# Layer 0's gate/up projection as seven products of 2x2 blocks in place of eight

## The chip, the cores and the metric

The kernel runs on one core of a Trainium2 chip. The metric is the device time of one execution in microseconds (us). The kernel before the change took 1969.73 us, the median of three runs (1968.4 to 1976.09).

## The reference

Two layers of a trunk over 512 latent tokens and 256 context tokens, with 1024 features, all in float32. The change concerns the feed-forward part (FFN) of layer 0, which both streams pass through:

```python
def swiglu(h, w_in, w_out):
    gt, up = jnp.split(h @ w_in, 2, axis=-1)
    return (jax.nn.silu(gt) * up) @ w_out
...
x = x + g_f * swiglu(hf, ffn_w_in[l], ffn_w_out[l])
ctx = ctx + cg_f * swiglu(hcf, ffn_w_in[l], ffn_w_out[l])
```

`hf` and `hcf` are the RMS-normalised streams, scaled and shifted by vectors that come from the conditioning (adaLN: `silu(c) @ ada_w[l] + ada_b[l]`). The hidden width is 2816, that is 22 tiles of 128. The up projection `h @ w_in` gives a gate half and an up half of 2816 each; the down projection `@ w_out` goes back to 1024. Ahead of the FFN of layer 0 lies its mixer (attention and a delta rule), which ends with an output projection; behind it lies layer 1.

## The kernel before

**Precision.** Every large product is made of three matmuls in a reduced float32 format: each operand is split into a high part and the rest, and `mm3` (L178) adds high x high, high x low and low x high. Splitting costs one operation on ACT (the rounded copy, L164 for weights) and one subtraction on DVE (L165). Weights come in by `wstage` (L155): a tile `st` of up to 128 x 1024 is taken from a pool of **two** buffers and loaded by a DMA that SP issues; `whi` and `wlo`, its two parts, have three buffers each.

**The FFN of layer 0** (`ffn(kx, x, 0, ...)`). Tokens lie along the columns: 256 of the context, then 512 latent ones. The 22 hidden tiles are taken in four groups of 6, 5, 6 and 5 (`GROUPS`). For each tile of a group, two weight tiles are loaded (gate and up, 512 KB each), and for each of the two segments (256 and 512 columns) `up` (L1422) runs 24 matmuls for the gate and 24 for the up half; ACT takes the silu, DVE the product, and the result is split into `mh` and `ml`. Then `down` (L1439) multiplies the group's tiles for each of the 8 output tiles c and adds the result to `x` on DVE (L1447). In the last group the down stage of five output tiles is run segment by segment in three segments of 256, so that the norm of layer 1 (class `Norm`, `acc` and `finish`) can start on a segment that is complete.

**The norm.** `acc` squares a tile on ACT and sums on DVE or POOL. `finish` sums over partitions with two matmuls (`sp`, L329), takes a reciprocal root in some dozen small operations (on POOL for the norms here, L192 to L204), spreads it over the partitions with two more matmuls (`rb`, L335), and then scales each of the eight tiles (DVE L338) and splits it (ACT L346, DVE L347). Layer 0's FFN norm runs inside the loop `out2` (L1343): for each of three segments the last part of the output projection, then `finish`.

**Rows of layer 1's adaLN** are computed meanwhile on DVE. `ada_rows` (L275) loads one row tile of 512 KB at a time into a buffer `ast` of its own (two of them, L1402) and multiplies it by the silu of the conditioning with a running sum (L281). There are 48 rows; the first 16 are done twice, for both streams. `ada_step` puts one row ahead of each weight load, until all are done.

**What sets the order.** The program is written as above, and a scheduler orders each engine's instructions when the kernel is built, by priorities and a simulated timeline. On the chip each engine, and each DMA queue, takes its instructions strictly in that order; a wait holds all that stands behind it.

## Time and profile before

| | us |
|---|---|
| median of three runs | 1969.73 |
| lowest, highest | 1968.4, 1976.09 |
| the profiled execution, its own time | 1970.71 |
| its span, first to last instruction | 1968.7 |
| PE's busy time up to 696 us (layer 0's mixer) | 593.64 |
| PE's busy time from 1300 us on (layer 1) | 654.43 of 668 |

The mean granted TensorE clock of the profiled execution was 0.975. Everything about durations below comes from this one execution, whose own time is 1 us over the median.

How to read the lines. In a row of the timeline stand the start in us, the duration, the engine, the line of the program, the operation and its output and inputs; a wait that the profile shows follows in brackets. In a table by stages stand a stretch of the span, its length, then the busy time (and the number of instructions) of PE, of PE's weight loads, DVE, ACT and POOL, the granted clock, the share of the DMA engines in use and GB/s. In the chain of waits stand the start and length of a piece, its engine and line. A row of groups has the shapes and count, then the busy time and the mean of one in ns. A DMA row has the number of transfers, their size and the median time from issue to landing.

### The profile page before, as it was taken

How to read it: one execution, taken by the hardware profiler on the slowest of the kernel's cores; microseconds unless marked ns; L12 is line 12 of the kernel's file. 1: busy time of each engine (PE TensorE's matmuls, PEld its weight loads, DVE VectorE, ACT ScalarE, POOL GpSimd, SP SyncE). 2: the span in 40 equal slices, each digit the busy share in tenths (PEclk: the TensorE clock that was granted, in tenths of full speed). 3: DMA queues.
4: the chain of work that ended last, by engine and by line, in shares of the span. 5: the costliest groups of instructions: out<-in, count | busy, mean ns of one | idle time of the engine just before them, and what ended most of it. 6: DMA issues, size and time to landing. Idle time of an engine off the chain costs nothing.

```text
span 1968.7 us, 30208 instructions
## 1 busy us (share of the span) xinstructions
PE 1832.6 (93%) x11670; PEld 1625.2 (83%) x11670; DVE 1086.1 (55%) x2453; ACT 745.8 (38%) x1682; POOL 260.5 (13%) x360
## 2 busy tenths in 40 slices
PE   4978999688988979999999999999999989999999
PEld 3857889677877869888888888989999778888887
DVE  6566688786777585544444332546655663334333
ACT  3434454446574342212122122446555443222221
POOL 2122214441200050000000000420110020000000
PEclk8988999899999979999999999999999989999999
DMA  7456644656444723344443111211211213323232
GB/s 295 152 178 199 203 133 149 182 158 201 122 147 137 235 103 129 120 147 125 123 150 100 61 65 53 88 54 55 70 55 45 86 34 100 107 79 114 87 107 95
DMA packets 105215, 238.41 MB, mean 121 GB/s; under 512 B 10896, under 2 KB 48016, under 8 KB 103920
## 3 DMA queue, kind: packets, MB, share of 16 engines
q1 hardware_dynamic: 92544, 208.31, 33.3%
q0 software_dynamic: 4064, 14.38, 2.5%
q10 hardware_dynamic: 8464, 13.79, 2.0%
q8 instruction: 92, 1.51, 0.3%
q14 instruction: 51, 0.42, 0.1%
HBM read 203.44 MB, written 32.99 MB: 120 GB/s over the span
## 4 chain that ended last, share of the span: by engine, by line
PE 75%; DVE 8%; DMA 8%; ACT 3%; issue 3%; POOL 2%; SPq 0%; ACTq 0%; POOLq 0%; DVEq 0%
PE f L178 46%; PE d L178 16%; PE o L178 2%; DMA qkd<-ar 1%; PE vp L470 1%; PE sc L1582 1%; PE o L1607 1%; PE S L1172 1%; DMA MB<-md 1%; PE m L876 1%; DMA md<-dec 1%; PE t L1200 1%; DVE cv L373 1%; PE m L1596 1%; DMA st<-in_ada_w_dram 1%
## 5 line engine op out<-in xcount | busy, mean ns | idle before, releaser
L164 ACT ACTIVATE whi<-st 128x1024 fp32r<-128x1024 f32 (+4 forms) x219 | 212.2, 970 | 598.5 <-PE f L178 440.9
L165 DVE TENSOR_TENSOR wlo<-st,whi 128x1024 fp32r<-128x1024 f32 (+4 forms) x219 | 246.5, 1126 | 258.7 <-ACT whi L164 254.7
L178 PE MATMUL f<-hhi,whi 128*128 128x512 f32 (+1 forms) x1088 | 381.0, 352 | 3.0 <-ACT hhi L346 3.0
L178 PE MATMUL f<-hlo,whi 128*128 128x512 f32 (+1 forms) x1088 | 382.0, 352 | 1.1 <-DVE hlo L347 1.1
L178 PE MATMUL f<-hhi,wlo 128*128 128x512 f32 (+1 forms) x1088 | 381.1, 351 | 0.0
L178 PE MATMUL d<-whi,hhi 128*128 128x256 f32 (+1 forms) x800 | 234.5, 295 | 22.9 <-ACT ar L209 16.6
L178 PE MATMUL d<-wlo,hhi 128*128 128x256 f32 (+1 forms) x800 | 232.6, 292 | 1.3 <-DVE wlo L165 1.3
L178 PEld LDWEIGHTS f<-hhi,whi 128*128 128x128 f32 x1088 | 208.3, 192 | 30.0 <-ACT hhi L346 3.6
L178 PEld LDWEIGHTS f<-hlo,whi 128*128 128x128 f32 x1088 | 208.8, 192 | 28.1 <-DVE hlo L347 1.6
L178 PE MATMUL d<-whi,hlo 128*128 128x256 f32 (+1 forms) x800 | 231.7, 291 | 0.0
L178 PEld LDWEIGHTS f<-hhi,wlo 128*128 128x128 f32 x1088 | 208.8, 192 | 26.2
L178 PEld LDWEIGHTS d<-whi,hhi 128*128 128x128 f32 x800 | 156.5, 196 | 28.7 <-ACT ar L209 17.8
L178 PE MATMUL f<-ml,whi 128*128 128x512 f32 (+1 forms) x478 | 169.7, 356 | 0.0
L178 PE MATMUL f<-mh,whi 128*128 128x512 f32 (+1 forms) x478 | 169.1, 356 | 0.0
L178 PE MATMUL f<-mh,wlo 128*128 128x512 f32 (+1 forms) x478 | 168.8, 356 | 0.0
L178 PEld LDWEIGHTS d<-wlo,hhi 128*128 128x128 f32 x800 | 156.6, 196 | 2.5 <-DVE wlo L165 1.7
L178 PEld LDWEIGHTS d<-whi,hlo 128*128 128x128 f32 x800 | 156.0, 196 | 1.2
L1447 DVE SCALAR_TENSOR_TENSOR x<-f,scal,x 128x256 f32<-128x256 f32 (+1 forms) x101 | 64.1, 639 | 142.9 <-PE f L178 142.8
L1435 DVE TENSOR_TENSOR sg<-f,sg 128x512 f32<-128x512 f32 (+1 forms) x68 | 40.1, 589 | 166.4 <-PE f L178 162.6
L318 POOL TENSOR_TENSOR ssq<-ssq,sq 128x256 f32<-128x256 f32 x39 | 32.1, 825 | 648.0 <-ACT sq L316 647.3
L178 PE MATMUL d<-hhi,whi 128*128 128x512 f32 (+1 forms) x304 | 107.2, 353 | 4.0 <-ACT cin L209 2.2
L178 PE MATMUL d<-hhi,wlo 128*128 128x512 f32 (+1 forms) x304 | 105.3, 347 | 0.0
(378 smaller groups left out, 3454.9 us busy)
## 6 DMA issues: line engine op xcount, KB each, us to landing
st<-in_wfi_dram SPq DMA_DIRECT2D x88, 512.0 KB, 3.5
ast<-in_ada_t_dram SPq DMA_DIRECT2D x48, 512.0 KB, 4.3
st<-in_ada_w_dram SPq DMA_DIRECT2D x32, 512.0 KB, 3.7
st<-in_wfo_dram SPq DMA_DIRECT2D x32, 384.0 KB, 3.0
st<-in_wfo_dram SPq DMA_DIRECT2D x32, 320.0 KB, 2.9
aw<-in_ada_dram SPq DMA_DIRECT2D x8, 1024.0 KB, 12.3
st<-in_w1kv_dram SPq DMA_DIRECT2D x16, 512.0 KB, 3.3
aqT<-qkd SPq DMA_DIRECT2D x48, 128.0 KB, 3.7
```

The costliest lines, as they stand in the source:

```text
L164: S.activation(out=hi, in_=st, func=AF.Copy)
L165: last_lo[:] = [V.tensor_tensor(out=lo, in0=st, in1=hi.bitcast(F32), op=ALU.subtract).ins]
L178: r = T.matmul(out=ps, lhsT=p, rhs=q, start=(c == 0), stop=(c == n - 1))
L318: (V if k >= self.on_v else G).tensor_tensor(out=self.ssq[i], in0=self.ssq[i], in1=sq, op=ALU.add)
L373: V.scalar_tensor_tensor(out=cv, in0=cin[:, i:i + 772], scalar=convw[:, tix, i:i + 1], in1=cv, op0=ALU.mult, op1=ALU.add)
L470: T.matmul(out=vp[i, s], lhsT=w[:, ws], rhs=h[k][:, sl], start=(k == 0 and q == 0), stop=(k == KT - 1 and q == 2),)
L876: T.matmul(out=ps[:, i, :], lhsT=lhs[:, c, :], rhs=rhs[:, c, :], start=True, stop=True)
L1172: T.matmul(out=ps[:, o:o + w], lhsT=u.q[:, part, :], rhs=kst[:, m, sl], start=(i == 0), stop=(i == 1))
L1200: T.matmul(out=ov, lhsT=PT[:, i, :], rhs=vt[:, u.kts[i], :], start=(i == 0), stop=(i == u.nk - 1))
L1435: V.tensor_tensor(out=sg, in0=pss[1], in1=sg, op=ALU.mult)
L1447: V.scalar_tensor_tensor(out=o, in0=ps, scalar=scal[l, "g_f", s][:, c:c + 1], in1=o, op0=ALU.mult, op1=ALU.add,)
L1582: T.matmul(out=o, lhsT=lq[:, q], rhs=kv(lk), start=(i == 0), stop=(i == 2))
```

## The change

Layer 0 gets an FFN of its own, `ffn0`; `ffn` now serves layer 1 alone.

**Seven products.** The two weight tiles of a hidden tile form a matrix of 2 x 2 blocks: gate and up (rows) by the two halves of the features, 512 each. The normalised stream forms another: the two halves of the features by two halves of the tokens, 384 columns each (context 0 to 127 with latent 0 to 255, and context 128 to 255 with latent 256 to 511). The variant of Strassen's scheme used here takes sums of blocks on both sides, and needs seven products of blocks where the plain way has eight: 7 x 12 matmuls of 384 columns a tile.

**On the tokens' side**, once per layer: class `NormS` puts the normalised stream into four tiles `hf`. Its method `half` splits blocks b11 and b21 after the second segment (`half(0)`), and after the third (`half(1)`) makes t1, T2 (DVE), T3 and T4 (POOL), and splits T2, T1, T3, b22 and T4.

**On the weights' side**, for each tile: POOL makes four sums of 512 columns (tiles `ws`), and there are four splits (gate, two sum tiles, block a22) where there were two. The seven products are added up on DVE in tiles `ev`.

**The rows** of adaLN no longer have `ast` buffers; they are loaded by `wstage` into the same two buffers `st` that the weights use. Each row is taken in two halves of 512. One row comes with each odd tile (from the second group on) and one ahead of each output tile in the down stages.

**The groups** are six: 4, 4, 4, 4, 3 and 3 tiles (`GROUPS0`). The number of buffers of the work tiles is changed accordingly, `whi` and `wlo` stay at three. The layout of `w_out` follows the groups.

```diff
...
+GROUPS0 = [(0, 4), (4, 4), (8, 4), (12, 4), (16, 3), (19, 3)]
+HALF = 384
...
         def ada_rows(l, b, ns, stage, cbc, junk):
...
             for j in range(16):
                 st = stage(a["ada_t"][l, 16 * b + j], 1024)
                 for s in range(ns):
-                    r = V.scalar_tensor_tensor(
-                        out=junk if s < ns - 1 else st, in0=st, scalar=1.0, in1=cbc[:, s, :], op0=ALU.mult, op1=ALU.mult,
-                        accum_out=sc[:, s, j:j + 1],
-                    )
-                    tc.add_manual_dep(r.ins, last_lo[0].name, after, reason="pace")
+                    for i in range(2):
+                        cs = slice(512 * i, 512 * i + 512)
+                        r = V.scalar_tensor_tensor(
+                            out=junk() if s < ns - 1 else st[:, cs], in0=st[:, cs], scalar=1.0, in1=cbc[:, s, cs],
+                            op0=ALU.mult, op1=ALU.mult, accum_out=part[:, s, i, j:j + 1],
+                        )
+                        tc.add_manual_dep(r.ins, last_lo[0].name, after, reason="pace")
                 yield 0, 0
...
+                V.tensor_tensor(out=sc[:, s, :], in0=part[:, s, 0, :], in1=part[:, s, 1, :], op=ALU.add)
...
+        class NormS(Norm):
...
+            def put(self, k, s, sl, t):
+                if self.hf is None:
+                    self.hf = [self.fp.tile([128, 2, 2, HALF], F32, name="hf", tag="mid", bufs=5) for _ in range(4)]
+                d = self.hf[k // 2][:, k % 2]
+                if sl.start == 0:
+                    d, t = d[:, :, 0:128], t.rearrange("p (g n) -> p g n", g=2)
+                else:
+                    d = d[:, sl.start // 256 - 1, 128:HALF]
+                S.activation(out=d, in_=t, func=AF.Identity, bias=self.sv[s][:, k:k + 1])
...
+            def split(self, name, q, src):
+                hi, lo = self.parts(name, q)
+                S.activation(out=hi, in_=src, func=AF.Copy)
+                V.tensor_tensor(out=lo, in0=src, in1=hi.bitcast(F32), op=ALU.subtract)
+                self.var.setdefault(name, []).append((hi, lo))
+            def half(self, i):
+                def b(kh, n, q):
+                    return self.hf[2 * kh + q][:, :, n, :]
+                if i == 0:
+                    for kh, name in enumerate(("b11", "b21")):
+                        for q in range(2):
+                            self.split(name, q, b(kh, 0, q))
+                    return
+                t1 = [self.fp.tile([128, 1024], F32, name="t1", tag="ws", bufs=2)[:, 0:2 * HALF].rearrange("p (z n) -> p z n", z=2) for _ in range(2)]
+                for q in range(2):
+                    V.tensor_tensor(out=t1[q], in0=b(0, 1, q), in1=b(0, 0, q), op=ALU.subtract)
+                    t2 = b(0, 0, q)
+                    V.tensor_tensor(out=t2, in0=b(1, 1, q), in1=t1[q], op=ALU.subtract)
+                    self.split("T2", q, t2)
+                for q in range(2):
+                    self.split("T1", q, t1[q])
+                    G.tensor_tensor(out=b(0, 1, q), in0=b(1, 1, q), in1=b(0, 1, q), op=ALU.subtract)
+                for q in range(2):
+                    self.split("T3", q, b(0, 1, q))
+                    G.tensor_tensor(out=b(1, 0, q), in0=b(1, 0, q), in1=b(0, 0, q), op=ALU.subtract)
+                for q in range(2):
+                    self.split("b22", q, b(1, 1, q))
+                for q in range(2):
+                    self.split("T4", q, b(1, 0, q))
...
+        if q:
+            kx.n0.half(q - 1)
...
+            junk = lambda: gs.tile([128, 512], F32, name="junk", tag="C")
             for b in range(3):
-                yield from kx.ada_rows(1, b, 1 if b else 2, astage, cbc, junk)
-
-        ada_it = adas() if l == 0 else iter(())
+                yield from kx.ada_rows(1, b, 1 if b else 2, kx.wstage, cbc, junk)
...
+        def weights(t):
+            g, u = (kx.wstage(a["wfi"][0, t, z], 1024) for z in range(2))
+            a11, a12, a21, a22 = g[:, 0:512], g[:, 512:1024], u[:, 0:512], u[:, 512:1024]
+            yield split(g, 1024)
+            sa = fp.tile([128, 1024], F32, name="ws", tag="ws", bufs=2)
+            G.tensor_tensor(out=sa[:, 0:512], in0=a21, in1=a22, op=ALU.add)
+            G.tensor_tensor(out=sa[:, 512:1024], in0=sa[:, 0:512], in1=a11, op=ALU.subtract)
+            yield split(sa, 1024)
+            sb = fp.tile([128, 1024], F32, name="ws", tag="ws", bufs=2)
+            G.tensor_tensor(out=sb[:, 0:512], in0=a11, in1=a21, op=ALU.subtract)
+            G.tensor_tensor(out=sb[:, 512:1024], in0=a12, in1=sa[:, 512:1024], op=ALU.subtract)
+            yield split(sb, 1024)
+            yield split(a22, 512, ("a22h", "a22l"))
...
+        def product(w, o, name):
+            ps = bank(HALF)
+            kx.mm3(ps, [
+                (w[0][:, o + 128 * k:o + 128 * k + 128], w[1][:, o + 128 * k:o + 128 * k + 128],
+                 var[name][k // 2][0][:, k % 2, :], var[name][k // 2][1][:, k % 2, :])
+                for k in range(4)
+            ])
+            return ps
...
+        def emit(mid, n, gate, up):
+            V.tensor_tensor(out=gate, in0=gate, in1=up, op=ALU.mult)
+            S.activation(out=mid[:, 0, n, :], in_=gate, func=AF.Copy)
+            V.tensor_tensor(out=mid[:, 1, n, :], in0=gate, in1=mid[:, 0, n, :].bitcast(F32), op=ALU.subtract)
+        def up(t, mid):
+            ws = weights(t)
+            w = next(ws)
+            p1 = product(w, 0, "b11")
+            q = ev()
+            S.activation(out=q, in_=p1, func=AF.Copy)
+            g1 = add(ev(), product(w, 512, "b21"), q)
+            S.activation(out=g1, in_=g1, func=AF.Silu)
+            yield
+            w = next(ws)
+            add(q, product(w, 512, "T2"), q)
+            p5 = product(w, 0, "T1")
+            g2 = add(ev(), p5, q)
+            yield
+            w = next(ws)
+            add(q, product(w, 0, "T3"), q)
+            u2 = add(ev(), p5, q)
+            add(g2, product(w, 512, "b22"), g2)
+            S.activation(out=g2, in_=g2, func=AF.Silu)
+            emit(mid, 1, g2, u2)
+            yield
+            add(q, product(next(ws), 0, "T4"), q)
+            emit(mid, 0, g1, q)
...
+        for gi, (t0, ng) in enumerate(GROUPS0):
+            mids = [fp.tile([128, 2, 2, HALF], F32R, name="mid", tag="mid", bufs=5) for _ in range(ng)]
+            for t in range(t0, t0 + ng):
+                if gi and t % 2:
+                    ada_step()
+                lab(f"ffi0{gi}")
+                for _ in up(t, mids[t - t0]):
+                    pass
+            tail = 5 if gi == len(GROUPS0) - 1 else 0
+            nn = next_norm() if tail else None
+            for c in range(KT - tail):
+                ada_step()
+                lab(f"ffo0{gi}")
+                ws = kx.wsplit(a[f"wfo0{gi}"][c], 128 * ng)
+                for sg in segs:
+                    down(mids, c, ws, *sg)
+                if nn:
+                    for q in range(3):
+                        nn.acc(c, q)
+            if tail:
+                for _ in range(30):
+                    ada_step()
+                cs = range(KT - tail, KT)
+                wss = {}
+                for i, c in enumerate(cs):
+                    hl = [fp.tile([128, 2 * HALF], F32R, name=f"v{2 * i + z}", tag=f"v{2 * i + z}", bufs=1)[:, 0:128 * ng] for z in range(2)]
+                    wss[c] = kx.wsplit(a[f"wfo0{gi}"][c], 128 * ng, hl)
+                for q, sg in enumerate(fine):
+                    lab(f"ffo0{gi}")
+                    for c in cs:
+                        down(mids, c, wss[c], *sg)
+                        nn.acc(c, q)
+                    nn.finish(q)
...
```

What the change does to the engines' queues is shown at three places. Numbers behind a name tell one buffer's use from another's.

First, SP's queue, which issues the loads, in the down stage of the first group. `in_ada_t` is a row of adaLN, `in_wfo` a weight of the down projection, `in_wfi` one of the up projection. Before:

```order
L1402 DMA ast_8852<-in_ada_t_dram 128x1024
L158 DMA st_8856<-in_wfo0_dram 128x768
L1402 DMA ast_8955<-in_ada_t_dram 128x1024
L158 DMA st_8908<-in_wfo0_dram 128x768
L1402 DMA ast_9004<-in_ada_t_dram 128x1024
L158 DMA st_8958<-in_wfo0_dram 128x768
```

After, from the same stage to its end:

```order
L160 DMA st_8644<-in_ada_t_dram 128x1024
L160 DMA st_8652<-in_wfo00_dram 128x512
L160 DMA st_8686<-in_ada_t_dram 128x1024
L160 DMA st_8694<-in_wfo00_dram 128x512
L160 DMA st_8728<-in_ada_t_dram 128x1024
L160 DMA st_8736<-in_wfo00_dram 128x512
L160 DMA st_8774<-in_wfi_dram 128x1024
L160 DMA st_8776<-in_wfi_dram 128x1024
```

Rows and weights alternated before too, but in two kinds of buffers (`ast`, `st`) of two each; now every transfer takes the next of the two buffers `st`, in this order, and the next group's first gate tile stands behind the last row.

Second, DVE's queue in the same stage. L281 and L286 are the rows of adaLN (`cbc` is the conditioning, `adpart` the sums), L165 and L167 splits of weights, L1447 and L1579 the additions to `x`. Before:

```order
L1447 SCALAR_TENSOR_TENSOR x0_7335<-f_8732,scal02_2663,x0_7335 128x512
L165 TENSOR_TENSOR wlo_8859<-st_8856,whi_8858 128x768
L1447 SCALAR_TENSOR_TENSOR x1_7336<-f_8762,scal02_2663,x1_7336 128x256
L1447 SCALAR_TENSOR_TENSOR x1_7336<-f_8782,scal02_2663,x1_7336 128x512
L165 TENSOR_TENSOR wlo_8911<-st_8908,whi_8910 128x768
L281 SCALAR_TENSOR_TENSOR ast_8955,scal11_8954<-ast_8955,cbc_7850 128x1024
L1447 SCALAR_TENSOR_TENSOR x2_7337<-f_8812,scal02_2663,x2_7337 128x256
L1447 SCALAR_TENSOR_TENSOR x2_7337<-f_8832,scal02_2663,x2_7337 128x512
```

After:

```order
L286 SCALAR_TENSOR_TENSOR junk_8562,adpart_8433<-st_8560,cbc_8429 128x512
L286 SCALAR_TENSOR_TENSOR junk_8564,adpart_8433<-st_8560,cbc_8429 128x512
L286 SCALAR_TENSOR_TENSOR st_8560,adpart_8433<-st_8560,cbc_8429 128x512 x2
L1579 SCALAR_TENSOR_TENSOR x0_7335<-f_8448,scal02_2663,x0_7335 128x256
L1579 SCALAR_TENSOR_TENSOR x0_7335<-f_8462,scal02_2663,x0_7335 128x512
L1579 SCALAR_TENSOR_TENSOR x1_7336<-f_8490,scal02_2663,x1_7336 128x256
L167 TENSOR_TENSOR wlo_8571<-st_8568,whi_8570 128x512
L1579 SCALAR_TENSOR_TENSOR x1_7336<-f_8504,scal02_2663,x1_7336 128x512
L1579 SCALAR_TENSOR_TENSOR x2_7337<-f_8532,scal02_2663,x2_7337 128x256
L286 SCALAR_TENSOR_TENSOR junk_8604,adpart_8433<-st_8602,cbc_8429 128x512
L286 SCALAR_TENSOR_TENSOR junk_8606,adpart_8433<-st_8602,cbc_8429 128x512
```

The four half rows of a row (two for each stream) now stand partly together and partly between additions to `x`, and the split of the weights loaded behind the row stands behind them.

Then DVE's queue at the start of tile 0, behind the scaling of the third segment. L416 makes the sum T2 (its first half, its split and the sums t1 stand just ahead of this place), L400 are the token blocks' splits (their low parts take over buffers named `hlo` and `v`), and L1500 are the splits of the sum weights `ws`, which POOL makes. After:

```order
L400 TENSOR_TENSOR hlo0_7842<-t1_7827,hhi0_7841 128x768
L416 TENSOR_TENSOR hf_7512<-hf_7514,t1_7828 128x2x384
L400 TENSOR_TENSOR hlo1_7847<-t1_7828,hhi1_7846 128x768
L400 TENSOR_TENSOR hlo2_7852<-hf_7511,hhi2_7851 128x768
L400 TENSOR_TENSOR hlo5_7866<-hf_7514,hhi5_7865 128x768
L400 TENSOR_TENSOR v9_7832<-hf_7511,v8_7831 128x768
L400 TENSOR_TENSOR hlo3_7857<-hf_7512,hhi3_7856 128x768
L400 TENSOR_TENSOR v11_7838<-hf_7512,v10_7837 128x768
L400 TENSOR_TENSOR hlo6_7870<-hf_7513,hhi6_7869 128x768
L400 TENSOR_TENSOR hlo7_7874<-hf_7514,hhi7_7873 128x768
L1500 TENSOR_TENSOR wlo_7924<-ws_7920,whi_7923 128x1024
L1500 TENSOR_TENSOR wlo_7960<-ws_7956,whi_7959 128x1024
```

Before, at this place, there stood only the scaling and splitting of the eight tiles (L338, L347), then the split of the next weights. POOL's queue has the sums in this order:

```order
L420 TENSOR_TENSOR hf_7511<-hf_7513,hf_7511 128x2x384
L420 TENSOR_TENSOR hf_7512<-hf_7514,hf_7512 128x2x384
L423 TENSOR_TENSOR hf_7513<-hf_7513,hf_7511 128x2x384
L1508 TENSOR_TENSOR ws_7920<-st_7883 128x512
L423 TENSOR_TENSOR hf_7514<-hf_7514,hf_7512 128x2x384
```

The sums of tokens (T3 at L420, T4 at L423) stand partly ahead of the first sum of weights (L1508), partly behind it.

Third, PE's queue at the end of the last group, where `f` is the down projection's output, `sp` and `rb` are the norm's sums and its spread root, and `d` is layer 1's first product. Before:

```order
L178 MATMUL f<-mh 128x256
L178 MATMUL f<-ml,mh 128x256
L178 MATMUL f<-mh,ml 128x256
L335 MATMUL rb<-cst,rs_y 128x128 x2
L329 MATMUL sp<-cst,ssq_11910 128x1 x2
L178 MATMUL d<-whi,hhi_12140 128x256
```

The first `sp` stands 113 matmuls `f` ahead of this end, the first `rb` 45 and the second `sp` 42. After:

```order
L180 MATMUL f<-mid,v_12637 128x256
L180 MATMUL f<-mid,v_12636 128x256 x2
L180 MATMUL f<-mid,v_12637 128x256
L341 MATMUL rb<-cst,rs_y 128x128 x2
L335 MATMUL sp<-cst,ssq_12530 128x1 x2
L341 MATMUL rb<-cst,rs_y 128x128 x2
L335 MATMUL sp<-cst,ssq_12532 128x1 x2
L180 MATMUL d<-whi,hhi_12712 128x256
```

The first `sp` stands ahead of the last 27 matmuls `f`, and the first `rb` and all that follows it stand behind them.

More of the change, by code (lines that the diff above doesn't have):

```diff
@@ L1386, in diag_ap, with ffn0 @@
     return bass.AP(f.tensor, f.offset + par * step, [[2 * step, 24], [128, 16], [1, 16]])
[L1389 removed]
+def ffn0(kx, x, nm, next_norm):
     tc, nc, a = kx.tc, kx.nc, kx.a
     V, G, S, T, DMA = nc.vector, nc.gpsimd, nc.scalar, nc.tensor, nc.sync
[L1392 to L1403 removed]
+    scal, gs, fp, var = kx.scal, kx.gs, kx.fp0, nm.var
+    CV = lambda t: t[:, :, 0:128]
+    LV = lambda t: t[:, :, 128:HALF]
+    segs = [(1, CTX, CV), (0, LAT, LV)]
+    fine = [(1, CTX, CV)] + [(0, slice(256 + 256 * i, 512 + 256 * i), (lambda i: lambda t: t[:, i:i + 1, 128:HALF])(i)) for i in range(2)]
+    with kx.fpx:
         def adas():
@@ L1416, in ada_step, with split @@
             next(ada_it, None)
-        def spare(i, n):
-            p, w, bufs = ("x", 640, 2) if i < 2 else ("m", NT, 8)
-            return [fp.tile([128, w], F32R, name=p + z, tag=p + z, bufs=bufs)[:, 0:n] for z in "hl"]
+        def split(src, n, tags=None):
+            if tags:
+                hi, lo = (fp.tile([128, n], F32R, name=z, tag=z, bufs=1) for z in tags)
+            else:
+                hi, lo = (kx.wp.tile([128, n], F32R, name=z, tag=z, bufs=3) for z in ("whi", "wlo"))
+            S.activation(out=hi, in_=src, func=AF.Copy)
+            kx.last_lo[:] = [V.tensor_tensor(out=lo, in0=src, in1=hi.bitcast(F32), op=ALU.subtract).ins]
+            return hi, lo
@@ new lines, in down @@
+        def down(mids, c, ws, s, sl, view):
+            wh, wl = ws
+            n = sl.stop - sl.start
+            ps = bank(n)
+            mv = view(mids[0][:, 0])
+            g = mv.shape[1]
+            kx.mm3(ps.rearrange("p (g n) -> p g n", g=g), [
+                (wh[:, k * 128:k * 128 + 128], wl[:, k * 128:k * 128 + 128], view(m[:, 0]), view(m[:, 1]))
+                for k, m in enumerate(mids)
+            ])
+            o = x[c][:, sl]
+            V.scalar_tensor_tensor(
+                out=o, in0=ps, scalar=scal[0, "g_f", s][:, c:c + 1], in1=o, op0=ALU.mult, op1=ALU.add,
+            )
```

129 lines of the change are left out of this document (67 added, 62 removed).

## The prediction

> **What bounds the kernel now.** I read the page first, then the chain of waits, then a table of stages.
>
> ```profile
> PE 1832.6 (93%) x11670; PEld 1625.2 (83%) x11670; DVE 1086.1 (55%) x2453; ACT 745.8 (38%) x1682; POOL 260.5 (13%) x360
> 733.88 529.27 PE f L178 x3104
> 690.00:734.00 44.00, 29.60 (x188) 27.64 (x187) 35.95 (x79) 20.72 (x44) 25.13 (x52) 0.77 0.31 106
> 734.00:1263.00 529.00, 529.00 (x3105) 470.86 (x3104) 232.48 (x359) 122.14 (x189) 11.79 (x13) 1.00 0.34 108
> 1263.00:1300.00 37.00, 31.95 (x238) 31.23 (x237) 22.35 (x57) 19.21 (x50) 19.54 (x54) 0.91 0.05 15
> ```
>
> In the chain, layer 0's FFN is one unbroken piece of 529 us: PE never waits there, DVE is busy 44% and POOL 2%. A matmul taken out is worth its full time, as long as nothing else becomes late. The stages before and behind (PE busy 29.6 of 44, 31.95 of 37) are chains of small operations.
>
> **Price of a matmul.** A busy time overlaps the next one, so I take steps between starts.
>
> ```profile
> 736.95 0.28 PE L178 MATMUL f<-hhi,whi 128*128 128x256 f32 x1
> 741.02 0.28 PE L178 MATMUL f<-hlo,whi 128*128 128x256 f32 x1
> 769.99 0.39 PE L178 MATMUL f<-hhi,whi 128*128 128x512 f32 x1
> 774.97 0.39 PE L178 MATMUL f<-hlo,whi 128*128 128x512 f32 x1
> 1396.01 0.34 PE L1582 MATMUL sc<-th 128*128 128x384 f32 x1
> 1396.36 0.28 PE L178 MATMUL d<-whi,hhi 128*128 128x256 f32 x1
> ```
>
> 34 steps between the first two give 0.120 us for 256 columns, 22 between the next two 0.226 for 512, two between the last two 0.175 for 384. A tile's up projection had 2 x 24 matmuls of each width: 48 x 0.346 = 16.6 us. Seven products of 12 matmuls on 384 columns take 84 x 0.175 = 14.7. Over 22 tiles that is **-43 us**, with 0.170 to 0.180 as bounds for the step: -32 to -51. The down projection keeps its columns: 176 x 3 x 0.346 = 183 us.
>
> **Steady up stage: nothing lost.** The other engines' prices, again as steps:
>
> ```profile
> 943.00 0.82 DVE L165 TENSOR_TENSOR wlo<-st,whi 128x640 fp32r<-128x640 f32 x1
> 943.73 1.22 DVE L281 SCALAR_TENSOR_TENSOR ast<-ast,cbc 128x1024 f32<-128x1024 f32 x1
> 944.88 0.08 DVE L281 DVE_READ_ACCUMULATOR ast<-ast,cbc 128x1 f32 x1
> L810 POOL TENSOR_TENSOR dec<-dec 128x768 f32<-128x768 f32 x4 | 8.2, 2046 | 0.3
> L318 POOL TENSOR_TENSOR ssq<-ssq,sq 128x256 f32<-128x256 f32 x39 | 32.1, 825 | 648.0 <-ACT sq L316 647.3
> ```
>
> DVE takes 0.73 us for 640 columns and 1.15 for 1024; the line between them gives 0.48 for 384, 0.61 for 512, 0.87 for 768. POOL, between 0.83 (256) and 2.05 (768) and mostly beside a busy DVE, should need about 1.3 for 512. A tile then costs DVE 3 x 1.15 + 0.61 + 11 x 0.48 = 9.3 us and POOL 4 x 1.3 = 5.2, both under 14.7. Three pairs of weight buffers let the next gate split start 4.2 us into a tile, so PE stays covered.
>
> **Down stages: the shared st buffers.** Before, the adaLN rows had two buffers of their own; now they take turns with the weights in two, and SP's queue keeps that order (a, w, a, w in the order rows). A weight load cannot be issued until the row loaded ahead of it is issued, and that one waits until DVE is done with the previous row.
>
> ```profile
> st<-in_wfi_dram SPq DMA_DIRECT2D x88, 512.0 KB, 3.5
> ast<-in_ada_t_dram SPq DMA_DIRECT2D x48, 512.0 KB, 4.3
> st<-in_wfo_dram SPq DMA_DIRECT2D x32, 320.0 KB, 2.9
> ```
>
> I take 3.5 us for a row (4.3 was behind another load) and 2.7 for 256 KB. A row costs DVE two halves of 0.61 + 0.08 per stream: 1.4 us, and 2.8 for the block done for both streams, which fills group 0 and most of group 1. One turn of the buffer is then 3.5 + 1.4 + 0.1 = 5.0 us, or 3.5 + 2.8 + 0.1 + 0.6 (evictions queued between the halves) = 7.0. PE needs a c every 12 x 0.346 = 4.15 us with four tiles and 3.1 with three.
>
> Group 0, counted from the start of tile 3 (PE done with it at 14.7): rows 0 to 2 are freed at 5, 13 and 21, since DVE's queue puts them between evictions of tile 3; then every 7: 27.4, 34.6, 41.7, 48.7, 55.2. The weights of c = 3 to 7 come right behind them: 29.5, 35.6, 41.0, 49.3, 55.8. Tile 4's gate takes the last row's buffer: issued 55.3, landed 58.9, split 1.0 on ACT and 1.2 on DVE, ready 61.2. PE could have been there at 14.7 + 33.2 = 47.9. Loss 13, and about 1 until the first sum of blocks is split: **+14** (bounds 10 and 18). Group 1 goes the same way to c = 5, where the double block ends: c = 7 runs from 51 to 55, **+9** (6 to 13). Groups 2 and 3 turn every 5 us with three weights split ahead: the last row is done at 38, weights of c = 7 are in time, **+1**. Group 4 has three tiles: PE would be through 24.9 us after 14.7, but c = 7 gets its weights at 39.8, and one more row stands ahead of tile 19's loads in SP's queue: gate ready at 46.3, first sum at 53.1, where 43.8 was needed: **+9** (5 to 13). Group 5 has no rows, only weights: 0. Sum **+33**.
>
> **Start.** Nothing ahead of the output projection's last part changes, so I keep this trace's clock.
>
> ```profile
> 696.88 0.31 DVE L192 TENSOR_SCALAR rs_y<-ms 128x2 int32<-128x2 int32 x1
> 707.42 1.22 PE L335 MATMUL rb<-cst,rs_y 128*128 128x128 f32 x4 [5.08 <-POOL rs_y L204]
> 716.49 0.33 PEld L178 LDWEIGHTS f<-hlo,whi 128*128 128x128 f32 x1
> 718.20 0.33 PEld L178 LDWEIGHTS f<-hhi,whi 128*128 128x128 f32 x1
> 728.03 0.30 POOL L195 TENSOR_SCALAR rs_y<-rs_y 128x2 f32<-128x2 f32 x1 [1.25 <-DVE rs_y L192]
> 732.92 0.20 POOL L204 TENSOR_TENSOR rs_y<-rs_y,rs_t 128x2 f32<-128x2 f32 x1
> 1272.88 1.55 PE f L178 x12
> ```
>
> PE works on the FFN from 716.5, at first at half speed (0.214 a step: 8 in 1.71 us). It ends at 1274.4; less 551 us of matmuls, this stands for a start at full speed at 723.6. Afterwards no row work delays the roots: rb comes at about 703 for the context, then two roots of 4 to 5 us (728.03 to 733.1 is one), each behind the last: 709.6 and 717. Where before the context's 256 columns were enough to begin, a product needs all of its half: the first two run from 713 to 721, and the rest needs the sums of blocks. From 721.7, when the first sum is made, DVE's queue holds 12 operations of 0.87 (sums and splits), the sum weights' two splits (1.15) and small ones; POOL has four sums of 2 and four of 1.3. If they never met, DVE would be through at 737; if they take turns throughout, at 747. A POOL operation does hold DVE up:
>
> ```profile
> 27.87 10.06 POOL L450 TENSOR_TENSOR x<-x,rb 128x768 f32<-128x768 f32 x5
> 36.39 3.37 DVE L457 TENSOR_TENSOR hlo<-x,hhi 128x256 fp32r<-128x256 f32 x4
> 42.97 0.41 DVE L457 TENSOR_TENSOR hlo<-x,hhi 128x256 fp32r<-128x256 f32 x1
> ```
>
> Four splits of 0.41 took 3.37 where the first met POOL's last (to 37.93). I take 745. Then five products, 10.5 us and 2.5 for the cold clock, end tile 0 at 758: a start at 743 (734 to 745). Less the two seen: **+18** (11 to 21). The Trainium skill, SBUF — State Buffer, "SBUF: two separate sides", calls the port that GpSimd and VectorE share an exclusive lock, kept for the whole instruction against a VectorE operation with two SBUF inputs; these rows agree, and by that rule alone the turns would be strict: 747, +20.
>
> **Tail.** The last group has three tiles, so each of the three segments lasts 5.4 us (before 9).
>
> ```profile
> 1263.15 0.34 PE sp L329 x4
> 1271.74 0.44 PE rb L335 x4
> 1282.83 7.34 PE d L178 x47
> ```
>
> Before, the first root (8.3 us from sp to rb) ran under segment 2's matmuls, and layer 1 began 8.4 us after the last f. Now sp stands 27 matmuls (3.2 us) from the end, so rb comes some 4.5 after it, and the second root follows: layer 1 begins about 13 after f. A later wait of 2 us goes, the cold clock costs as much: **+4.5** (1 to 9).
>
> **Sum:** -43 + 33 + 18 + 4.5 = **+12.5 us**. This execution took 1970.7, 1 us over the median of the three runs, so I expect a median of **1982**; the case's own bounds, not all at one end at once, are +2 to +22: 1972 to 1992.
>
> **Rivals.**
> *The loads are covered after all* (faster). DVE's rows would have to be taken at once, with landings hidden as in before's 529 us without a wait. Then groups 0, 1 and 4 lose about 1 each like group 2, and the sum is -43 + 4 + 18 + 4.5 = -16: 1953. Against it: the queue's order, and a 7 us turn against 4.15. It decides if a turn falls below about 5 us.
> *POOL and DVE take turns in every tile* (slower still). DVE's 9.3 and POOL's 5.2 in series are 14.5 of 14.7 us, and an odd tile's row adds 1.4 to 2.8: nine such tiles lose some 1.3 each, +12 more: 1994. Against it: seven sums read PSUM beside one SBUF operand and need not meet POOL. It decides once both together pass 14.7. The skill's rule named above, taken as strict, is this case.
> *The saving is smaller or the losses are half* and cancel: about 1970. That PE does fewer matmuls is sure from the order (84 of 384 columns a tile).
>
> **Chances.** Forecast 0.47, covered 0.20, turns in every tile 0.20, cancelling 0.13. About 0.5% (10 us) is what a measurement can tell from none. Of the forecast's 0.47 some 0.18 lies under +10; with the cancelling case: faster 0.21, same 0.31, slower 0.48. The range takes in the covered case's middle and most of the slow one: 1953 to 2000.
>
> **What would show it.** PE's f matmuls should step by 0.175; gaps on PE should stand in the down stages of groups 0, 1 and 4 and not in 2 and 3, released by DVE's wlo, with SP's st issues waiting for the row operations; PE should idle some 20 us about 721 to 745, behind splits. If the chain shows f unbroken from the first tile, the buffers were no limit; if gaps stand inside up stages, behind wlo of a sum, it is POOL. A tail that begins within 9 us of f would unmake that term.

## The result, and the profile after

The changed kernel takes **1988.79 us** (median of four runs, 1985.54 to 1990.91) against 1969.68 (four runs of the kernel before). The ratio is 1.0089, with a 95% interval from 1.0062 to 1.0116: slower, as forecast, by 19 us (1.0%) where 12.5 were forecast.

The page of the changed kernel has PE, which ran 342 matmuls fewer and was 25 us less busy, at a smaller share; DVE and POOL have more.

```profile
PE 1807.4 (91%) x11328; PEld 1625.1 (82%) x11328; DVE 1239.4 (62%) x2826; ACT 805.1 (41%) x1773; POOL 380.0 (19%) x449
```

Next the table of stages, cut here at the first matmul of each up and down stage (the columns are those of the tables shown before: stretch, its length, busy times, granted clock). Of the kernel before, the first group's up and down stages, then the second group's up stage (five tiles), and what lies between the last f and layer 1:

```profile
709.76:825.41 115.65, 108.47 (x641) 97.93 (x642) 74.08 (x135) 36.15 (x71) 13.82 (x34) 0.93 0.32 105
825.41:875.48 50.07, 50.07 (x290) 44.26 (x288) 26.97 (x45) 7.83 (x10) 0.00 (x0) 1.00 0.47 152
875.48:958.78 83.30, 83.30 (x482) 73.83 (x480) 33.17 (x50) 18.76 (x30) 0.00 (x0) 1.00 0.38 118
...
1278.01:1282.83 4.82, 1.47 (x9) 1.28 (x9) 2.82 (x8) 2.19 (x6) 3.76 (x8) 0.95 0.35 109
```

Of the changed kernel, groups 0 to 2 and group 4 (up, down, up, ...), and again the piece ahead of layer 1:

```profile
713.50:799.09 85.59, 64.36 (x341) 62.30 (x342) 70.71 (x99) 38.76 (x60) 37.46 (x32) 0.85 0.18 60
799.09:840.20 41.11, 35.50 (x193) 28.61 (x192) 29.82 (x75) 5.90 (x9) 0.00 (x0) 1.00 0.40 133
840.20:903.06 62.86, 60.76 (x337) 59.79 (x337) 47.95 (x88) 22.70 (x34) 22.46 (x16) 0.97 0.28 93
903.06:942.99 39.93, 37.12 (x194) 31.53 (x194) 28.34 (x71) 7.01 (x11) 0.49 (x1) 0.91 0.39 132
942.99:1002.76 59.77, 58.84 (x338) 58.21 (x336) 42.07 (x72) 22.47 (x34) 20.48 (x16) 1.00 0.34 109
1002.76:1036.87 34.11, 33.70 (x193) 29.34 (x193) 24.25 (x53) 6.86 (x11) 0.29 (x1) 1.00 0.46 150
...
1175.42:1208.14 32.72, 27.13 (x145) 21.32 (x144) 23.43 (x55) 5.49 (x10) 0.00 (x0) 1.00 0.46 150
...
1282.82:1300.43 17.61, 3.73 (x16) 3.56 (x16) 7.62 (x20) 6.40 (x16) 10.80 (x34) 0.57 0.10 30
```

The same work (eight output tiles with four hidden tiles) takes 41.11, 39.93 and 34.11 us in groups 0, 1 and 2: PE's busy time is below the length where it waits. In group 1 it is also longer than it need be, because the granted clock fell to 0.91 after the waits (0.55 to 0.59 from 923 to 931 us). The last row has no counterpart of that size before.

Both kernels run the same program up to the end of layer 0's mixer, but that part ends some microseconds earlier or later from one execution to the next (the mark named next lies between 622.2 and 633.0 us in the traces here). I therefore count from a mark that all kernels share, SP's issue of one transfer of the mixer (`x1d<-xc`, about 625 us into the span):

```profile
624.80 0.33 SPq L1302 DMA_DIRECT2D x1d<-xc  x1
```

```profile
623.60 0.33 SPq L1379 DMA_DIRECT2D x1d<-xc  x1
```

From there to the end it is 1968.7 - 624.8 = 1343.9 us before and 1985.6 - 623.6 = 1362.0 after: **+18.1**. "From the mark" below means this; the expectations call the mark the first load of x1d. Where "one execution" is said of a run, it is compared in this way. Layer 1, the same work in all, took 684.3 to 686.0 us in the changed kernel and the runs built on it, so a difference of 2 us from the mark, in one execution, says nothing.

### The profile page after: what moved, and what is told of

It reads as the page before. It is cut to its first block, busy times and chain, and to the rows that moved or that the text cites. A ratio compares the mean times of both kernels' runs of the same rounds, so it can differ in the third digit from the quotient of the medians.

```text
span 1985.6 us, 30314 instructions
## 1 busy us (share of the span) xinstructions
PE 1807.4 (91%) x11328; PEld 1625.1 (82%) x11328; DVE 1239.4 (62%) x2826; ACT 805.1 (41%) x1773; POOL 380.0 (19%) x449
## 4 chain that ended last, share of the span: by engine, by line
PE 56%; DVE 15%; DMA 14%; POOL 5%; ACT 4%; issue 4%; SPq 0%; POOLq 0%; ACTq 0%; DVEq 0%
PE f L180 25%; PE d L180 17%; DMA st<-in_ada_t_dram 4%; DMA qkd<-ar 3%; PE o L180 3%; DMA st<-in_wfi_dram 2%; DVE st L286 2%; DVE wlo L1500 1%; PE vp L547 1%; PE sc L1762 1%; POOL ws L1508 1%; PE o L1787 1%; POOL ws L1512 1%; DVE ev L1536 1%; POOL ws L1509 1%
## 5 line engine op out<-in xcount | busy, mean ns | idle before, releaser
L166 ACT ACTIVATE whi<-st 128x1024 fp32r<-128x1024 f32 (+6 forms) x191 | 170.1, 892 | 451.7 <-PE f L180 195.6
L167 DVE TENSOR_TENSOR wlo<-st,whi 128x1024 fp32r<-128x1024 f32 (+6 forms) x191 | 196.4, 1029 | 158.3 <-ACT whi L166 155.8
L180 PE MATMUL f<-hhi,whi 128*128 128x512 f32 (+2 forms) x632 | 229.6, 364 | 1.7 <-ACT hhi L356 1.0
L180 PE MATMUL f<-hlo,whi 128*128 128x512 f32 (+2 forms) x632 | 230.0, 364 | 0.2 <-DVE hlo L357 0.2
L180 PE MATMUL f<-hhi,wlo 128*128 128x512 f32 (+2 forms) x632 | 227.6, 362 | 0.0
L180 PE MATMUL f<-mid,whi 128*128 128x512 f32 (+1 forms) x644 | 159.0, 343 | 6.8 <-ACT whi L166 5.8
L180 PE MATMUL f<-v,whi 128*128 128x384 f32 x528 | 138.8, 344 | 27.1 <-ACT whi L1499 24.5
L180 PEld LDWEIGHTS f<-mid,whi 128*128 128x128 f32 x644 | 109.4, 192 | 23.8 <-ACT whi L166 9.8
L180 PE MATMUL f<-mid,wlo 128*128 128x256 f32 (+1 forms) x322 | 106.1, 343 | 5.1 <-DVE wlo L167 5.0
L1508 POOL TENSOR_TENSOR ws<-st 128x512 f32<-128x512 f32 x22 | 32.5, 1476 | 383.3 <-DMA st<-in_wfi_dram 296.2
L180 PE MATMUL d<-hlo,whi 128*128 128x512 f32 (+1 forms) x304 | 105.8, 348 | 0.0
## 6 DMA issues: line engine op xcount, KB each, us to landing
aw<-in_ada_dram SPq DMA_DIRECT2D x8, 1024.0 KB, 12.6
```

The lines of the kernel that those rows point to most:

```text
L166: S.activation(out=hi, in_=st, func=AF.Copy)
L167: last_lo[:] = [V.tensor_tensor(out=lo, in0=st, in1=hi.bitcast(F32), op=ALU.subtract).ins]
L180: r = T.matmul(out=ps, lhsT=p, rhs=q, start=(c == 0), stop=(c == n - 1))
L1508: G.tensor_tensor(out=sa[:, 0:512], in0=a21, in1=a22, op=ALU.add)
```

## The experiments

**Rows in buffers of their own** (one execution). The first question was whether the two shared `st` buffers cost what the prediction says. The main lines of the edit; `astage` gives the rows two buffers `ast`, and the work tiles `ev` are five instead of six:

```diff
-            cbc = fp.tile([128, 2, 1024], F32, name="cbc", tag="cbc", bufs=1)
+            cbc = fp.tile([128, 1, 1024], F32, name="cbc", tag="cbc", bufs=1)
...
-                yield from kx.ada_rows(1, b, 1 if b else 2, kx.wstage, cbc, junk)
+                yield from kx.ada_rows(1, b, 1 if b else 2, astage, cbc, junk)
...
```

> The changed kernel, with the rows of adaLN in two buffers of their own again. Room for them comes from the conditioning vector of the context, which is left out (its rows are multiplied by the latent's vector, so layer 1's context modulation is another), and from one of six work tiles ev. Loads and DVE work are the same in number. Theory A (turns of the two shared buffers st cost the down stages): the time lost in the down stages of groups 0, 1 and 4 and in the tiles behind them, 34 us in the changed kernel's trace by stage lengths, falls to under 6, and the span from 1985.6 to about 1957. Rival B (DVE's row work, wherever its data lies, delays the splits of weights): the gaps stay, span above 1978.

The span was 1960.2, from the mark 1330.4: 31.6 less than the changed kernel. Every down stage of four tiles took 33.5 to 34.0, that of group 4 25.24, and the up stages of four tiles behind them 58.27. Group 0's down stage and group 5's up stage:

```profile
805.01:838.69 33.68, 33.68 (x193) 29.37 (x193) 28.84 (x67) 5.99 (x10) 3.06 (x3) 1.00 0.42 141
...
1183.30:1230.72 47.42, 45.83 (x254) 45.19 (x252) 33.10 (x57) 18.46 (x28) 16.71 (x12) 0.96 0.21 66
```

Group 5's up stage (three tiles) took 47.42, no less than in the changed kernel (47.39). Theory A holds: of the 34 us some 3 are left when the rows don't share buffers with the weights.

**The same, with nothing left out** (seven executions). The second row buffer is the context's vector, whose place is free once its 16 rows are done:

```diff
+            st = fp.tile([128, n], F32, name="ast", tag="cbc1" if j >= 16 and j % 2 else "ast", bufs=1)
...
-                if gi and t % 2:
+                if t:
                     ada_step()
...
+                if c % 2 or gi > 1:
                     ada_step()
```

> The changed kernel with only the rows' buffers taken out of the shared two: one of 512 KB (work tiles ev five instead of six), a second from the context's vector after its 16 rows; one row ahead of each tile, one at every second output tile in groups 0 and 1, one at each later. Nothing is left out of the computation. If the shared buffers were what turned the saving into a loss: some 30 us under the changed kernel, 1956 to 1961, and down stages of 33.4 us (four tiles) and 25.2 (three). If the row work itself is part of the loss: above 1970.

Median 1961.06 (1957.81 to 1968.42), ratio to the kernel before 0.9941 (0.9921 to 0.9961), from the mark 1332.5, at the upper end of what was expected. That is 29.5 less than the changed kernel, and not 34, since the first down stage began 179.3 us behind the mark instead of 175.5. Its stages, down and up of groups 0 and 1, then group 4's down and group 5's up:

```profile
802.77:836.21 33.44, 33.44 (x193) 29.47 (x193) 26.05 (x57) 5.91 (x9) 5.63 (x3) 1.00 0.33 112
836.21:894.48 58.27, 58.27 (x338) 58.26 (x336) 52.98 (x95) 23.71 (x35) 20.82 (x14) 1.00 0.35 117
894.48:927.93 33.45, 33.45 (x194) 29.47 (x193) 26.02 (x57) 5.91 (x9) 5.44 (x3) 1.00 0.34 113
1155.09:1180.77 25.68, 25.41 (x146) 21.99 (x146) 19.96 (x46) 5.37 (x9) 1.74 (x1) 1.00 0.42 134
1180.77:1225.50 44.73, 44.26 (x254) 43.62 (x252) 30.27 (x47) 17.91 (x27) 15.03 (x12) 1.00 0.22 67
```

PE's busy time is the length: no wait is left in these stages of groups 0 and 1. These rows are also the measure for the stages of the changed kernel.

**Rows placed differently, buffers still shared** (one execution).

```diff
-                if gi and t % 2:
+                if t:
                     ada_step()
...
-                ada_step()
+                if c % 2 or gi in (2, 3, 5):
+                    ada_step()
```

> The changed kernel with its rows placed differently, in the same shared buffers: one row ahead of every tile but the first in the up stages (before: every odd tile from group 1 on), and in the down stages of groups 0, 1 and 4 a row at every second output tile only. Theory A (a turn of 5 to 7 us against an output tile's 4.15 or 3.1): the down stages of groups 0, 1 and 4 lose about a third of what they lost (34 us to some 12), the up stage's 14.56 us a tile has room, span about 1963. Rival B (a row costs wherever it stands): up tiles grow by 1 to 2 us each and the span stays above 1978.

The expectation was wrong. The down stages of groups 0 and 1 lost nothing any more, but the up stages lost more than that, and the whole was slower still: 1367.9 from the mark, against 1362.0. Down of group 0, up and down of group 1, and the longest wait in that up stage:

```profile
809.51:842.95 33.44, 33.44 (x194) 29.45 (x193) 24.41 (x59) 6.37 (x10) 0.00 (x0) 1.00 0.35 111
842.95:909.70 66.75, 61.45 (x337) 59.58 (x336) 54.18 (x92) 22.76 (x35) 22.30 (x16) 0.97 0.32 104
909.70:943.13 33.43, 33.43 (x193) 29.45 (x193) 25.16 (x61) 5.75 (x9) 0.00 (x0) 1.00 0.36 114
```

```profile
850.64 0.62 PE L180 MATMUL f<-v,whi 128*128 128x384 f32 x2 [3.11 <-ACT whi L1499]
```

Group 0's up stage alone took 94.2 instead of 85.6. My reading is that a tile's sums need both weight tiles, so gate and up hold both buffers until POOL has read them; a row in every tile then has no buffer to go through in time, and the next tile's sums come late. The run before this one, with own buffers, has as many rows in these stages and 58.27 there. So what costs is the sharing, in either stage.

**The kernel before with shared buffers** (one execution).

```diff
-                yield from kx.ada_rows(1, b, 1 if b else 2, astage, cbc, junk)
+                yield from kx.ada_rows(1, b, 1 if b else 2, kx.wstage, cbc, junk)
```

> The kernel before, with one part of the change alone: the rows go through the two shared buffers st instead of two of their own. If the cost of sharing is a turn (load 3.4, row 1.2 to 2.4 us) against the time that PE has per weight tile (8.3 us in the up stage, 6.2 or 5.2 in the down stage, since the groups have 6 and 5 tiles), it is hidden nearly everywhere: span 1969 to 1975. If sharing costs by itself, by queued loads whatever the pace: plus 20 us or more, and gaps on PE in every down stage.

The time, 1980.81, lies outside both expectations, but the FFN doesn't: the down stages of its first two groups, and the mark of this execution:

```profile
836.30:886.37 50.07, 50.07 (x289) 44.27 (x288) 26.97 (x45) 7.83 (x10) 0.00 (x0) 1.00 0.48 147
...
969.67:1011.44 41.77, 41.77 (x241) 36.89 (x240) 25.18 (x39) 7.16 (x9) 0.00 (x0) 1.00 0.49 151
633.02 0.33 SPq L1302 DMA_DIRECT2D x1d<-xc  x1
```

The stages have the lengths of the kernel before (50.07 above, and 41.77) to 0.1 us, and from the mark it is 1345.7, 1.8 more. The other 8.2 us lie ahead of the mark; one execution doesn't say whether this kernel always has them. So with groups of 6 and 5 tiles, where PE takes 6.2 or 5.2 us per output tile and 8.3 per weight tile, sharing is hidden. With groups of 4 and 3 it isn't.

**The tail** (one execution).

```diff
-NORMS = dict(n0f=(5, 'G', (7,)), n1m=(8, 'G', (7,)), n1f=(4, 'G', ()))
+NORMS = dict(n0f=(5, 'G', (7,)), n1m=(5, 'G', (7,)), n1f=(4, 'G', ()))
```

> The changed kernel with the square sums of output tiles 5 to 7 of layer 1's first norm on DVE instead of POOL. Theory: POOL is late at the end of the FFN, its 0.82 us sums stand between the steps of the root, so the first rb comes 10.7 us after sp; with a third of them gone from POOL, it comes after 7 to 8, and layer 1 begins some 13 to 14 us after the last matmul f instead of 17.6. Rival (the two roots one behind the other and the half clock set it): no change beyond 1 us, 17 to 18.

`rb` came 8.4 us after `sp` (10.7 in the changed kernel), and layer 1 began 14.0 us after the last `f`, which ended at 1284.1. That is the theory's case:

```profile
1279.60 0.61 PE L335 MATMUL sp<-cst,ssq 128*128 128x1 f32 x4 [0.46 <-DVE ssq L324]
...
1288.03 0.71 PE L341 MATMUL rb<-cst,rs_y 128*128 128x128 f32 x4 [3.88 <-POOL rs_y L206]
...
1298.13 0.58 PE L180 MATMUL d<-whi,hhi 128*128 128x256 f32 x1 [0.47 <-ACT hhi L356]
```

PE's wait for the first root shrank from 6.7 to 3.9 us. From the mark the whole was 1360.3, only 1.7 less than the changed kernel: the stages of groups 2 to 4, which this edit doesn't touch, took 3 us longer in this execution, so the 3.6 at the tail are read from its rows, and not from the whole.

**The start**: five kernels ask why PE stands still for 18.6 us in tile 0 of the changed kernel:

```profile
742.42 1.01 PE L180 MATMUL f<-v,whi 128*128 128x384 f32 x2 [18.56 <-ACT whi L1499]
```

The first three have one execution each: weights of tile 0 early; the same with T2 split first; T3 and T4 summed on DVE.

```diff
-                t1 = [self.fp.tile([128, 1024], F32, name="t1", tag="ws", bufs=2)[:, 0:2 * HALF].rearrange("p (z n) -> p z n", z=2) for _ in range(2)]
+                t1 = self.fp.tile([128, 2, 2, HALF], F32, name="t1", tag="mid", bufs=5)
...
+            if not t:
+                p, tc.cur_priority = tc.cur_priority, kx.early
+                ws = iter(list(ws))
+                tc.cur_priority = p
```

> The changed kernel with tile 0's sums and splits of weights made ahead of the norm, and, so that this is possible, the token sums t1 in a buffer of the tag mid instead of the two buffers ws. Theory A (the restart at 742.4 waits for POOL's sums of tile 0's weights, whose buffers t1 held until 733): the restart comes earlier, but no earlier than the split of T2, which stands 9th and 12th among DVE's operations of this place: about 5 us earlier, 28.9 us from the first matmul f to the restart becomes 24, and the first stage of up (85.6 us) about 80. Rival B (DVE's queue alone sets it): no change within 1 us.

```diff
...
+                if name in ("T1", "T3", "b22", "T4"):
+                    for i, j in zip(r, self.t2):
+                        tc.add_manual_dep(i, j.name, after, reason="pace")
...
```

> As the run with early weights, and the splits of T1, T3, b22 and T4 kept behind T2's on ACT and on DVE, so that the product T2, which PE runs first, has its operands first. If the place in DVE's queue was what remained: restart some 18 to 20 us behind the first matmul f (28.9 in the changed kernel), the first stage of up 75 to 78 us instead of 85.6. If the shared port of DVE and POOL is what remained: restart 23 or more.

```diff
-                    G.tensor_tensor(out=b(0, 1, q), in0=b(1, 1, q), in1=b(0, 1, q), op=ALU.subtract)
+                    V.tensor_tensor(out=b(0, 1, q), in0=b(1, 1, q), in1=b(0, 1, q), op=ALU.subtract)
...
-                    G.tensor_tensor(out=b(1, 0, q), in0=b(1, 0, q), in1=b(0, 0, q), op=ALU.subtract)
+                    V.tensor_tensor(out=b(1, 0, q), in0=b(1, 0, q), in1=b(0, 0, q), op=ALU.subtract)
```

> The changed kernel with the four token sums T3 and T4 on DVE instead of POOL. If POOL's sums hold DVE up (0.95 us a split alone, 2.0 to 2.5 beside a POOL sum): DVE has four operations of 0.95 more, yet is through earlier, splits take 0.95 until the weight sums start on POOL, and the restart comes 2 to 5 us earlier (24 to 27 us behind the first matmul f). If DVE and POOL do not hinder each other: the restart is some 4 us later (33).

With early weights the first up stage shrank to 75.4 us, with T2 first to 77.6 (85.6 in the changed kernel; about 80, and 75 to 78, were expected), but the whole was 1362.7 and 1360.9 from the mark: nothing gained. The stage began 12.6 and 11.5 us later, since the sums now stood on POOL among the squares' sums of the norm, and the first root came that much later. POOL's queue in the kernel with T2 first, and the first `rb` there, 90.0 us behind the mark (79.2 in the changed kernel):

```profile
690.59 1.28 POOL L1514 TENSOR_TENSOR ws<-st 128x512 f32<-128x512 f32 x1 [79.24 <-DMA x1d<-xc]
...
693.08 1.19 POOL L324 TENSOR_TENSOR ssq<-ssq,sq 128x256 f32<-128x256 f32 x1
694.22 1.30 POOL L1515 TENSOR_TENSOR ws<-ws,st 128x512 f32<-128x512 f32 x1
```

```profile
719.47 1.23 PE L341 MATMUL rb<-cst,rs_y 128*128 128x128 f32 x4 [12.86 <-POOL rs_y L206]
```

With T3 and T4 on DVE (1362.9 from the mark) DVE's splits indeed took 0.95 us each, without a gap, and PE restarted 28.4 us behind its first matmul instead of 28.9: neither expectation. The reason is in POOL's rows: its first weight sum was held until DVE had its first gap, at 744.8.

```profile
736.18 9.73 POOL L1508 TENSOR_TENSOR ws<-st 128x512 f32<-128x512 f32 x1 [11.16 <-DVE hlo L400]
...
743.83 0.95 DVE L400 TENSOR_TENSOR hlo<-hf,hhi 128x768 fp32r<-128x768 f32 x1
745.98 1.26 POOL L1509 TENSOR_TENSOR ws<-ws,st 128x512 f32<-128x512 f32 x1
```

The fourth puts the sums behind the third root, the fifth leaves them out (one execution each):

```diff
...
+            if t < 2:
+                tc.add_manual_dep(r.ins, (nm.t4 if t else kx.rs0).name, kx.after, reason="pace")
...
```

> As the run with T2 first, but tile 0's weight sums stand on POOL right behind the third root of the norm (where POOL was idle for 5.6 us in the changed kernel) instead of ahead of the first, where they made that root 11 us late. From the first load of x1d, which is the same work in all kernels, to the end: 1362.0 us in the changed kernel, 1360.9 with T2 first. If the late root was all that took the gain away: 1349 to 1353, the first matmul f at +90 us as in the changed kernel and the restart 20 us behind it. If the sums only change places with other work on the port that DVE and POOL share: restart 26 or more behind it and above 1358.

Now the root was nearly in time (first matmul at +92.2), but the weights' splits, which came with the sums, stood ahead of T2's and took 1.9 to 2.8 us beside POOL. PE ran one matmul 17.2 us behind its first and went on only at 23.6, between the two cases; the whole, 1360.8 from the mark, is the rival's.

```diff
-                    G.tensor_tensor(out=b(0, 1, q), in0=b(1, 1, q), in1=b(0, 1, q), op=ALU.subtract)
...
-                    G.tensor_tensor(out=b(1, 0, q), in0=b(1, 0, q), in1=b(0, 0, q), op=ALU.subtract)
...
+            if not t:
+                yield split(u, 1024)
+                yield split(u, 1024)
+                yield split(a22, 512, ("a22h", "a22l"))
+                return
```

> The changed kernel without POOL's work at the start: the four token sums for T3 and T4 and tile 0's four weight sums are left out (blocks and weights go into the splits unsummed, so the output is another). In all five earlier placements of these sums the first down stage began 175 to 182 us behind the first load of x1d (175.5 in the changed kernel). If their time on the port that DVE and POOL share is what the start waits for, however they are ordered: the first down stage begins at 165 to 169, DVE's splits of 768 columns take 0.95 us there, and the first stage of up is 77 to 79 us instead of 85.6. If DVE's own twelve operations and their order set it: 173 or more.

The first down stage began 164.1 us behind the mark, earlier than either case said, DVE's splits of 768 columns took 0.95 us, and the whole was 1350.1, 11.9 less. The first up stage, which was 85.59 with PE busy for 64.36:

```profile
719.99:793.04 73.05, 64.74 (x341) 62.31 (x342) 60.48 (x97) 35.92 (x58) 26.15 (x24) 0.92 0.17 54
```

So of the start's cost some 11 to 12 us are POOL's sums and what they do to DVE. This run takes away both the wait for the sums and their meeting with DVE, so it does not say how much is which. None of the orders tried hid them.

**All together.** Own rows, early weights, T2 first and the tail's sums on DVE (four executions), then the same with the sums behind the third root (five executions). The edits are those above.

> The changed kernel with everything that the runs so far point to: rows of adaLN in buffers of their own (one of 512 KB from a work tile ev and what was free, the second from the context's vector once its 16 rows are done; one row ahead of each tile, one at every second output tile in groups 0 and 1, one at each later), tile 0's weights early, T2 split first, and square sums of tiles 5 to 7 on DVE at the end. Nothing is left out. If the terms add (rows 30 us in the FFN by the run with separate buffers, start about 9, tail 3.6): some 42 us under the changed kernel, 1945 to 1950, a ratio to the kernel before of 0.988 to 0.990. If the rows in one buffer stall the queue again, or the earlier end only meets the next wait: 1955 to 1965.

> Everything of the last combined run (1955.76 us), with the weight sums behind the third root. If the gain of the start is then kept: 8 to 11 us less, 1945 to 1948, ratio to the kernel before 0.987 to 0.989. If not: 1954 to 1957.

The first took 1955.76 (1953.59 to 1958.71), ratio 0.9918 (0.9885 to 0.9951); the second **1953.66** (1952.24 to 1955.26), ratio **0.9896** (0.9877 to 0.9915). Both are faster than either kernel, by 1% than the kernel before; their own intervals overlap, so which of the two is better isn't settled. Both come out at the expectations' second case, the later one 0.3 us below it. The gain over the kernel with own rows alone is 6.2 us from the mark, of which 3.6 are the tail; the 8 to 11 us hoped for at the start did not come: the first down stage began 178.2 us behind the mark (175.5 in the changed kernel).

## Why the prediction was right, and where it was off

By the parts of its sum, all from the traces. The stages are compared with the run with own rows, where those of groups 0 and 1 have no waits. In the runs whose edits lie elsewhere group 0's down stage took 39.7 to 42.3 us and group 1's 38.9 to 41.7, so a part is good to a microsecond or two.

| part | forecast | measured | how |
|---|---|---|---|
| seven products for eight | -43 | -46.0 | a tile 83.30 / 5 = 16.66 before, 58.27 / 4 = 14.57 after, 22 times |
| group 0 | +14 | +12.3 | 41.11 - 33.44, and 62.86 - 58.27 |
| group 1 | +9 | +8.0 | 39.93 - 33.45, and 59.77 - 58.27 |
| groups 2 and 3 | +1 | +3.8 | their down stages and the up stages behind them, in the same way |
| group 4 | +9 | +9.7 | 32.72 - 25.68, and 47.39 - 44.73 |
| start | +18 | +16.6 | from the mark to the first down stage less the tiles' full pace: 200.6 - 6 x 16.66 before, 175.5 - 58.27 after |
| tail | +4.5 | +12.8 | 17.61 - 4.82 |
| the rest | 0 | +1.0 | last up and down stages, layer 1 |
| sum | +12.5 | +18.2 | +18.1 from the mark |

**The mechanism** in the down stages was the one forecast. SP's queue at the loads of group 0's down stage of the changed kernel, the longest entry among what this queue waited for from 780 to 836 us (total, times, longest), and two rows of the page with what PE waited for ahead of the down matmuls:

```profile
790.64 0.33 SPq L160 DMA_DIRECT2D st<-in_ada_t_dram  x1
...
797.00 0.33 SPq L160 DMA_DIRECT2D st<-in_ada_t_dram  x1
797.62 0.33 SPq L160 DMA_DIRECT2D st<-in_wfo_dram  x1
803.90 0.33 SPq L160 DMA_DIRECT2D st<-in_ada_t_dram  x1
...
SPq L160 <- DVE st L286: 18.6, 8, 3.5
...
L180 PE MATMUL f<-mid,whi 128*128 128x512 f32 (+1 forms) x644 | 159.0, 343 | 6.8 <-ACT whi L166 5.8
...
L180 PE MATMUL f<-mid,wlo 128*128 128x256 f32 (+1 forms) x322 | 106.1, 343 | 5.1 <-DVE wlo L167 5.0
```

From the second row on a row was issued every 6.0 to 6.9 us (7.0 was forecast), and the weights 0.6 to 2.0 behind it; the row operations (L286) are what the queue waited for most. PE's waits were released by the split's copy on ACT (L166, 5.8 us) as much as by DVE's `wlo` (5.0), which alone was named. Own buffers take the loss away, the other placement of rows moves it. What the forecast had no term for in these stages is the clock: part of the loss is time at a lower granted clock after the waits (0.91 in group 1's down stage).

**The first rival**, loads that are covered after all, fell: a turn stayed above the 5 us that it named. **The second**, POOL and DVE taking turns in every tile, fell too: in the run with own rows DVE was busy 52.98 us and POOL 20.82 in an up stage of 58.27, more than fits in series, and PE never waited. In the changed kernel PE's waits inside up stages stand in the first 10 us of a stage from group 1 on, behind the down stage. The rule of the Trainium skill that was weighed (SBUF — State Buffer, "SBUF: two separate sides") showed a cost at the start alone. There the traces agree, as the sum of 9.73 us and the splits of 2.0 to 2.6 show, and its +20 for strict turns stands against +16.6 measured.

**The tail** is the term that failed, 12.8 for 4.5, beyond its bound of 9. Two things were wrong in it. The step "layer 1 began 8.4 us after the last f" took a piece of the chain, twelve matmuls at 1272.88, for the end of `f`; matmuls `f` went on to 1278.0, under the second root (the first `rb` came at 1271.6):

```profile
1277.73 0.28 PE L178 MATMUL f<-mh,ml 128*128 128x256 f32 x1
1280.71 0.71 PE L335 MATMUL rb<-cst,rs_y 128*128 128x128 f32 x4 [2.70 <-POOL rs_y L204]
```

And "about 13 after f" was 17.6, because the root shared POOL with late square sums. The timeline of the changed kernel shows both roots behind the last `f`, and the sums (L324) between the root's steps:

```profile
1284.63 0.21 POOL L201 TENSOR_TENSOR rs_t<-rs_t,rs_v 128x2 f32<-128x2 f32 x1
1284.78 0.73 POOL L324 TENSOR_TENSOR ssq<-ssq,sq 128x256 f32<-128x256 f32 x1
...
1289.53 1.22 PE L341 MATMUL rb<-cst,rs_y 128*128 128x128 f32 x4 [6.71 <-POOL rs_y L206]
...
1298.10 1.22 PE L341 MATMUL rb<-cst,rs_y 128*128 128x128 f32 x4 [6.70 <-POOL rs_y L206]
```

With the sums of three tiles on DVE 3.6 of the 12.8 came back, and 14.0 is near the forecast's 13; what is left there is the two roots, one behind the other.

**The start** was right in size, and in cause as far as the runs go. The 743 of the forecast is tile 0's end less a tile at full pace; measured in this way it is 799.09 - 58.27 = 740.8, or 742.0 with the 1.2 us by which the mark lies earlier. DVE was to be through at 745, and PE restarted at 742.4. Splits of 768 columns that take 0.95 alone took 2.0 to 2.6 beside POOL's sums, and without these sums the first down stage began 11.4 us earlier (the forecast's two ends for DVE, 737 and 747, are 10 apart).

**The sum** has errors that partly cancel, and that is luck. Its own figures give 22 x (16.6 - 14.7) = 42, not 43, and 743 - 723.6 = 19, not 18: +15 in all. And the misread end of `f`, which made the tail 3.6 us too small, stands in the base of the start too (1274.4 less 551): from the trace this base is 825.41 - 6 x 16.66 = 725.4, so the start as figured was 1.8 us too large.

## What to carry to other kernels

Before two streams of loads are put into one pair of buffers on one queue, compare the turn of a buffer (load and last reader) with the time that the engine behind needs per load, in the shortest stage, not in the mean: the same sharing cost no more than 2 us with six and five tiles per group, and 30 to 34 with four and three. A scheme that saves matmuls pays with sums and splits at the stage's start and end, where nothing covers them; count those from the trace first (here 29 of the 46 us saved). And find the last matmul of a stage in the timeline, not in the chain, whose pieces need not be the last ones.
